# A two-layer hybrid decoder on one core: small products placed singly among large ones, lambda computed later, the rotation fed from a copy, and the compressed weights split by VectorE

## The chip, the core and the metric

The kernel runs on one core of a Trainium2 chip. A core has TensorE (PE, with the weight loads shown apart as PEld), VectorE (DVE), ScalarE (ACT), GpSimd (POOL) and SyncE (SP), which issues the transfers; matrix products are written to PSUM, everything else lies in SBUF. The metric is the device time in microseconds of one execution; less is better.

## The reference

Two layers; in each, a normalised input h is projected once, and three mixers work on the pieces: (A) sparse attention with compressed, selected and window branches, (B) differential attention with two softmax maps a head and a learned lambda, (C) a chunked spatial-gating unit. Their outputs are projected, gated and merged, then a SwiGLU feed-forward follows.

```python
q_a, kv_a, g_a, q_b, k_b, v_b, uv_c = jnp.split(h @ w_in[l], IN_OFFSETS, axis=-1)
# A: compressed branch, then selected blocks and the window (both see every earlier key here: 512 tokens)
p_c = masked_softmax(einsum(q, kc) * scale, cmp_end <= t);  o_cmp = p_c @ vc
out = gb[..., 0:1] * o_cmp + gb[..., 1:2] * o_slc + gb[..., 2:3] * o_win
# B
lam = exp(sum(lq1 * lk1)) - exp(sum(lq2 * lk2)) + lambda_init
o = rmsnorm((p[:, :, 0] - lam * p[:, :, 1]) @ v, subln_g) * (1.0 - lambda_init)
# C
u * (tril(w_s) @ rmsnorm(v) + b_s)
# merge and feed-forward
x = x + (gates_a * (o_a @ w_a) + gates_b * (o_b @ w_b) + gates_c * (o_c @ w_c)) @ w_out
x = x + (silu(h @ w1) * (h @ w3)) @ w2
```

Sizes: 512 tokens, D_MODEL 1024, 8 heads of 64 in two groups for A, 4 double heads for B, feed-forward width 2816, float32.

## The kernel before

Every large product is done in three parts (`mm3`, lines 184 to 186): weights and activations are each split into a rounded high part and the rest, and high x high, low x high, high x low are summed in one PSUM bank, 128 weights columns by 512 tokens each. The V projections run the other way round (`tm`, lines 224 to 226), with 280 or 512 columns. Weights come in chunks of 128 x 1024; `chunk` and `ahead` load them five ahead and split them two ahead: high part by ScalarE (line 163), low part by VectorE (line 166), or by GpSimd for 512 columns of a chunk during the gate products.

The small products are those of the mixers: in the selected and window attention (`nsa`) logits `sA` (lines 878 and 879), transposes of the probabilities `sB` (line 936, 128 columns, two or four at a time), products with V `sC` (lines 958 and 969); in the differential attention (`diff`) the same three (lines 878, 1050, 1061); in the spatial gating `prod` (line 764); in the compressed softmax (`cmp_soft`) the logits `s0` (line 812) and transposes `s4` (line 849). 

The order of work is written by `run`. A list of tasks (projections, gates, branches, feed-forward) yields after each three-part product with an estimate of its time, 650 ns. Two lanes of generators (lane 0: rotation tables, compression, spatial gating, compressed softmax, lambda; lane 1: `nsa` and `diff`) are given that time and step until they have used it up; each step emits its instructions at once and yields a weight. `later` postpones work by a number of ticks, `later_ns` by estimated time. Below this the framework may still move instructions on an engine. Each engine works through its queue in order.

Four banks' names matter: PSUM tiles tagged `g` (three banks, large products), `s` (two, logits and gating), `t` (two, transposes and compressed logits) and `o` (one). A tile's bank is free again when its last reader is done. `rope_pair` rotates a projection: `fa` and `fb` multiply the two halves in PSUM by cosine and sine (lines 663, 664, 673, 674) and, for the sparse attention's queries, keep a raw copy (lines 668, 677, 679); the two halves of QA1 use the copy on VectorE at line 679. `lambdas` (lines 461 to 472) computes lambda, half of the merge biases and a scale, for both layers.

## Time and profile before

| what | value |
|---|---|
| median of 3 runs | 1770.16 us (1769.95 to 1770.19) |
| the profiled execution's own time | 1770.18 us |
| its span, first to last instruction | 1768.3 us |
| granted TensorE clock, mean | 0.999 |
| TensorE products, busy | 1755.5 us, 99%, 8436 records |
| VectorE, ScalarE, GpSimd busy | 968.9, 751.4, 354.0 us |
| DMA | 205.78 MB, mean 116 GB/s |
| TensorE waiting for the raw copy (line 679) | 2.5 us in 2 waits |

Rows of the timeline read: start in us from the span's start, length, engine, line, operation, output <- inputs, shape, count, and in brackets the idle time before it with what ended it. PE is a product, PEld the load of its stationary operand. The ends of products are modelled: 0.39 us for 512 columns, while the next one starts sooner. The list of waits reads: who waited, for whom, us in all, times, the longest.

### The profile page before, as it was taken

What the parts mean: (1) busy time and instruction counts of PE and PEld (TensorE: products, weight loads), DVE (VectorE), ACT (ScalarE), POOL (GpSimd) and SP (SyncE); (2) the same over time, 40 slices, a digit from 0 to 9 for tenths busy, and PEclk for the clock granted to TensorE, in tenths of its full rate; (3) what the DMA queues carried; (4) which work ended last, traced back from release to release, by engine and by line L of the source; (5) the groups of instructions that cost most, each with busy time, mean ns of one, the idle gap of its engine ahead of it and who ended that gap; (6) DMA issues with size and microseconds to landing.
All of it is one profiled execution on the core that took longest, in us unless ns stands there. A gap on an engine that the chain in (4) does not pass through costs nothing.

```text
span 1768.3 us, 22696 instructions
## 1 busy us (share of the span) xinstructions
PE 1755.5 (99%) x8436; PEld 1465.0 (83%) x8436; DVE 968.9 (55%) x1774; ACT 751.4 (42%) x1317; POOL 354.0 (20%) x355
## 2 busy tenths in 40 slices
PE   9999999999999999999999999999999999999998
PEld 7888888888888888888888888888888888888887
DVE  6877665665644444433366786746656444444223
ACT  6557663444333332222244576634533333322222
POOL 0244332444120000000012343214430200000000
PEclk9999999999999999999999999999999999999999
DMA  7571126532322222223344612255413232222221
GB/s 259 190 221 68 54 72 185 173 120 90 113 96 96 96 95 96 96 99 125 109 145 146 220 47 68 80 171 161 149 66 114 95 107 96 96 95 96 100 101 50
DMA packets 67726, 205.78 MB, mean 116 GB/s; under 512 B 8992, under 2 KB 9376, under 8 KB 67616
## 3 DMA queue, kind: packets, MB, share of 16 engines
q1 hardware_dynamic: 67472, 204.29, 34.6%
q8 instruction: 67, 1.10, 0.3%
q14 instruction: 43, 0.35, 0.1%
q10 hardware_dynamic: 144, 0.04, 0.0%
HBM read 185.29 MB, written 19.01 MB: 116 GB/s over the span
## 4 chain that ended last, share of the span: by engine, by line
PE 97%; DVE 1%; ACT 1%; DMA 0%; issue 0%; POOL 0%; SPq 0%; DVEq 0%; ACTq 0%; POOLq 0%
PE ps_g L184 26%; PE ps_g L185 26%; PE ps_g L186 26%; PE ps_o L958 2%; PE ps_t L936 2%; PE ps_s L879 2%; PE ps_g L224 2%; PE ps_s L878 2%; PE ps_g L225 2%; PE ps_g L226 2%; PE ps_o L1061 1%; DVE wl L166 1%; PE ps_o L226 1%; PE ps_o L224 1%; PE ps_o L225 0%; PE ps_t L1050 0%
## 5 line engine op out<-in xcount | busy, mean ns | idle before, releaser
L163 ACT ACTIVATE wh<-wr 128x1024 fp32r<-128x1024 f32 (+2 forms) x320 | 315.4, 989 | 654.2 <-PE ps_g L186 351.7
L184 PE MATMUL ps_g<-xg,wh 128*128 128x512 f32 x1400 | 553.8, 396 | 0.0
L185 PE MATMUL ps_g<-xg,wl 128*128 128x512 f32 x1400 | 546.8, 391 | 0.0
L186 PE MATMUL ps_g<-xg,wh 128*128 128x512 f32 x1400 | 546.2, 390 | 0.1
L166 DVE TENSOR_TENSOR wl<-wr,wh 128x1024 fp32r<-128x1024 f32 (+1 forms) x308 | 367.5, 1195 | 234.8 <-ACT wh L163 231.3
L186 PEld LDWEIGHTS ps_g<-xg,wh 128*128 128x128 f32 x1400 | 262.8, 188 | 56.2 <-DVE xg L283 1.0
L184 PEld LDWEIGHTS ps_g<-xg,wh 128*128 128x128 f32 x1400 | 263.2, 188 | 50.4 <-ACT xg L280 0.5
L185 PEld LDWEIGHTS ps_g<-xg,wl 128*128 128x128 f32 x1400 | 263.3, 188 | 49.0 <-DVE wl L290 0.3
L869 ACT ACTIVATE e<-e,nm 128x384 f32<-128x384 f32 (+2 forms) x192 | 107.2, 559 | 89.0 <-DVE nm L867 85.0
L184 PE MATMUL ps_g<-act,wh 128*128 128x512 f32 (+1 forms) x374 | 141.2, 378 | 0.0
L185 PE MATMUL ps_g<-act,wl 128*128 128x512 f32 (+1 forms) x374 | 140.8, 376 | 0.0
L186 PE MATMUL ps_g<-act,wh 128*128 128x512 f32 (+1 forms) x374 | 140.8, 376 | 0.0
L497 POOL TENSOR_TENSOR acc<-acc,sq 128x512 f32<-128x512 f32 x18 | 29.3, 1626 | 433.6 <-ACT sq L496 433.6
L919 POOL TENSOR_SCALAR e<-e,sm,ga 128x128 f32<-128x128 f32 (+3 forms) x128 | 82.1, 652 | 111.8 <-DVE sm L915 88.7
L867 DVE CUSTOM_DVE_ANT_0 e<-ps_s,con 128x384 f32<-128x384 f32 (+2 forms) x192 | 90.8, 483 | 22.3 <-PE ps_s L879 20.7
L1202 DVE TENSOR_TENSOR fb<-ps_g,R 128x512 f32<-128x512 f32 x44 | 30.4, 691 | 129.1 <-PE ps_g L186 129.1
L166 POOL TENSOR_TENSOR wl<-wr,wh 128x512 fp32r<-128x512 f32 x48 | 72.6, 1513 | 117.7 <-ACT wh L163 117.7
L1193 DVE TENSOR_TENSOR fa<-ps_g,R 128x512 f32<-128x512 f32 x44 | 30.4, 691 | 95.7 <-PE ps_g L186 95.7
L186 PEld LDWEIGHTS ps_g<-act,wh 128*128 128x128 f32 x374 | 70.3, 188 | 13.0
L184 PEld LDWEIGHTS ps_g<-act,wh 128*128 128x128 f32 x374 | 70.3, 188 | 12.9
L185 PEld LDWEIGHTS ps_g<-act,wl 128*128 128x128 f32 x374 | 70.4, 188 | 12.8
L945 DVE TENSOR_TENSOR pt<-ps_t,pt 128x512 fp32r<-128x512 f32 (+1 forms) x96 | 56.7, 597 | 27.4 <-ACT pt L937 27.2
(248 smaller groups left out, 2474.2 us busy)
## 6 DMA issues: line engine op xcount, KB each, us to landing
wr<-in_wst SPq DMA_DIRECT2D x266, 512.0 KB, 3.3
rp_d<-pc SPq DMA_DIRECT2D x112, 128.0 KB, 3.6
wr<-in_wst SPq DMA_DIRECT2D x52, 256.0 KB, 2.6
q<-rp_d SPq DMA_DIRECT2D x16, 512.0 KB, 5.9
kh<-rp_d SPq DMA_DIRECT2D x24, 256.0 KB, 5.8
xT<-in_xT SPq DMA_DIRECT2D x7, 512.0 KB, 6.2
kl<-rp_d SPq DMA_DIRECT2D x12, 256.0 KB, 6.8
xtok<-in_xtok SPq DMA_DIRECT2D x4, 512.0 KB, 8.7
```

The lines of the kernel that those rows point to most:

```text
L163: nc.scalar.activation(h[:, :w], t[:, :w], AF.Copy)
L166: eng.tensor_tensor(lo[:, a:b], t[:, a:b], h[:, a:b].bitcast(F32), op=OP.subtract)
L184: nc.tensor.matmul(out, wh[:, c], xh[:, ts], start=first, stop=False)
L185: nc.tensor.matmul(out, wl[:, c], xh[:, ts], start=False, stop=False)
L186: nc.tensor.matmul(out, wh[:, c], xl[:, ts], start=False, stop=last)
L224: nc.tensor.matmul(o, x[k][:, 0, ts], wh[:, sl], start=(k == 0), stop=False)
L225: nc.tensor.matmul(o, x[k][:, 0, ts], wl[:, sl], start=False, stop=False)
L226: nc.tensor.matmul(o, x[k][:, 1, ts], wh[:, sl], start=False, stop=(k == KT - 1))
L867: nc.vector.tensor_tensor_reduce(out=e[:, :n], in0=s[:, :n], in1=self.mask[:, S - n:], scale=-0.125, scalar=3e38, op0=OP.add, op1=OP.min, ...
L869: nc.scalar.activation(e[:, :n], e[:, :n], AF.Exp, bias=nm, scale=-1.0, accum_out=sm)
L919: nc.gpsimd.tensor_scalar(e[:, :n], e[:, :n], sm[:, h:h + 1], self.ga[:, i, b:b + 1], op0=OP.mult, op1=OP.mult)
L945: nc.vector.tensor_tensor(lo, pt, hi.bitcast(F32), op=OP.subtract)
```

## The change

The diff makes five edits.

1. `mm3` becomes a generator that yields after each of its products (`BIG` = 650/3 ns), and so do `tm`, `prod`, `s0`, `s4`, both `sB`, and in `diff` `sC` and the first logits. The last part of the second layer's feed-forward calls `mm3` without these stops. A yield of a tuple counts time but is no tick (`tick(..., step)`), so work postponed by ticks is due as before. With it lanes can put one small product between two large ones. The weights that lanes yield elsewhere are cut so that a unit's sum is about the same.
2. `lambdas` is divided: biases and scale (`scales`) come with the rotation tables, lambda itself goes behind the first compressed softmax in lane 0; what needed it (gates of C before) becomes KB1.
3. In `fb`, for QA1, the raw copy comes first, and the two products read the copy in SBUF instead of PSUM.
4. In `cmp_soft` the high part of the compressed weights is copied by VectorE in `s5`, just ahead of the low part, and no longer by ScalarE in `s4`.
5. Weights of steps change (W_NSA, W_DIFF shares, 1300 for lambda).

```diff
--- before.py
+++ after.py
@@ -32,6 +32,7 @@
 W_NSA, W_DIFF, LAG = 470, 1200, 4
+BIG = 650 / 3
 WARM = 14
@@ -117,8 +118,9 @@

-    def tick(self, ns=0):
-        self.now += 1
+    def tick(self, ns=0, step=1):
+
+        self.now += step
         self.clock += ns
@@ -182,7 +184,9 @@
         nc.tensor.matmul(out, wh[:, c], xh[:, ts], start=first, stop=False)
+        yield BIG,
         nc.tensor.matmul(out, wl[:, c], xh[:, ts], start=False, stop=False)
+        yield BIG,
         nc.tensor.matmul(out, wh[:, c], xl[:, ts], start=False, stop=last)
@@ -198,14 +202,14 @@
                 outs[m] = self.bank(tag)
-            self.mm3(outs[m], w, x, k, k, k == 0, k == K - 1)
+            yield from self.mm3(outs[m], w, x, k, k, k == 0, k == K - 1)
             if (late and ((m == 0 and k == 5) or (m and k == K - 1))) or (not late and k == 3):
...
                 evacs[m](outs[m])
-            yield 650
+            yield BIG

...
@@ -447,12 +453,27 @@

+    def scales(self):
+
+        nc = self.nc
+        first = len(nc.cur_bb.bb.instructions)
+        self.bh, self.sub = [], []
+        for l in range(L):
+            bh = self.const(f"bh{l}", [P, 24])
+            nc.vector.tensor_scalar(bh, self.par[l][:, P_BM:P_BM + 24], 0.5, None, op0=OP.mult)
+            self.bh.append(bh)
+            sub = self.const(f"sub{l}", [P, 1])
+            nc.vector.tensor_scalar(sub, self.par[l][:, P_SUB:P_SUB + 1], 0.2 + 0.6 * math.exp(-0.3 * l), None,
+                                    op0=OP.mult)
+            self.sub.append(sub)
+        self.holds.append((first, len(nc.cur_bb.bb.instructions)))
+
     def lambdas(self):
...
         lq = self.lq.rearrange("p (l f d) -> p l f d", l=L, f=4)
-        self.nlam, self.bh, self.sub = [], [], []
+        self.nlam = []
         for l in range(L):
@@ -465,14 +486,8 @@
             self.nlam.append(nl)
-            bh = self.const(f"bh{l}", [P, 24])
-            nc.vector.tensor_scalar(bh, self.par[l][:, P_BM:P_BM + 24], 0.5, None, op0=OP.mult)
-            self.bh.append(bh)
-            sub = self.const(f"sub{l}", [P, 1])
-            nc.vector.tensor_scalar(sub, self.par[l][:, P_SUB:P_SUB + 1], 1.0 - li, None, op0=OP.mult)
-            self.sub.append(sub)
         self.holds.append((first, len(nc.cur_bb.bb.instructions)))
-        yield 300
+        yield 1300

@@ -670,13 +685,13 @@
             t2, t3 = self.t2("t2"), self.t2("t3")
+            if raw == 1:
+                nc.vector.tensor_copy(st["raw"][:, 1, :], ps)
+                ps = st["raw"][:, 1, :]
             nc.vector.tensor_tensor(t2, ps, self.sinR, op=OP.mult)
             nc.vector.tensor_tensor(t3, ps, self.cosR, op=OP.mult)
-            if raw is not None:
-                if raw == 0:
-                    nc.scalar.activation(st["raw"][:, 1, :], ps, AF.Copy)
-                else:
-                    nc.vector.tensor_copy(st["raw"][:, 1, :], ps)
+            if raw == 0:
+                nc.scalar.activation(st["raw"][:, 1, :], ps, AF.Copy)
             o1, o2 = st["t1"], st["t4"]
@@ -763,7 +778,8 @@
                                  start=True, stop=True)
-            return ps
+                yield BIG,
+            pss[t] = ps

@@ -788,8 +804,8 @@
             if t < TT:
-                pss[t] = prod(t)
-                yield 1300
+                yield from prod(t)
+                yield 450
                 tmps[t] = mix(t, pss.pop(t))
...
@@ -847,15 +864,18 @@
                 nc.tensor.transpose(pt[:, t * P:(t + 1) * P], st["ef"][:, t, :], self.ident)
-            pc = self.PcT[g] = self.t4("pcT", [P, 2, S], F32R)
-            nc.scalar.activation(pc[:, 0, :], pt, AF.Copy)
+                yield BIG,
+            self.PcT[g] = self.t4("pcT", [P, 2, S], F32R)

...
             pc = self.PcT[g]
+            nc.vector.tensor_copy(pc[:, 0, :], st["pt"])
             nc.vector.tensor_tensor(pc[:, 1, :], st["pt"], pc[:, 0, :].bitcast(F32), op=OP.subtract)

-        for w, f in (((2600 * (g == 0), lambda: None), (1300, s0), (1300, s1), (1300, s2), (2600, ex)), ((2600, s3), (2600, s4), (1300, s5)))[part]:
-            f()
+        for w, f in (((2600 * (g == 0), lambda: None), (450, s0), (1300, s1), (1300, s2), (2600, ex)), ((2600, s3), (450, s4), (1300, s5)))[part]:
+            parts = f()
+            if parts is not None:
+                yield from parts
             yield w
@@ -934,6 +954,7 @@
                     nc.tensor.transpose(pt[:, j - 2 * part, h, :], E[2 * v + h][:, j * P:(j + 1) * P], self.ident)
+                    yield BIG,
             nc.scalar.activation(hi, pt[:, 0:len(js)], AF.Copy)
@@ -1000,16 +1021,16 @@
                 sA(u)
-            yield W_NSA
+            yield W_NSA * 0.6
             w = u - b
...
             if w % 2 and ok(w):
-                sB(w // 2, 0)
+                yield from sB(w // 2, 0)
             elif w % 2 == 0 and ok(w - 2):
-                sB(w // 2 - 1, 1)
+                yield from sB(w // 2 - 1, 1)
             if w % 2 == 0 and ok(w - 4):
                 sC(w // 2 - 2)
-            yield W_NSA
+            yield W_NSA / 4
         self.ensure("oa")
@@ -1023,7 +1044,12 @@
             n = (i + 1) * P
-            s = self.logits(q2[c][:, j], kh[c][:, j, :n], kl[c][:, j, :n], i)
+            ts = slice(i * P, n)
+            s = self.bank("s")
+            nc.tensor.matmul(s[:, :n], q2[c][:, j, ts], kh[c][:, j, :n], start=True, stop=False)
+            if i == 0:
+                yield BIG,
+            nc.tensor.matmul(s[:, :n], q2[c][:, j, ts], kl[c][:, j, :n], start=False, stop=True)
             E[u, j] = self.soft(s, (i + 1) * P, i)
...
@@ -1104,18 +1132,18 @@
             if ok(u):
-                sA(u, 0)
-            yield W_DIFF
+                yield from sA(u, 0)
+            yield W_DIFF * 0.75
             if ok(u):
-                sA(u, 1)
+                yield from sA(u, 1)
             if ok(u - 2):
                 sM(u - 2)
-            yield W_DIFF
+            yield W_DIFF * 0.75
             if ok(u - 3):
-                sB(u - 3)
+                yield from sB(u - 3)
             if ok(u - 4):
-                sC(u - 4)
-            yield W_DIFF
+                yield from sC(u - 4)
+            yield W_DIFF * 0.5
         if p == 1:
@@ -1172,7 +1200,7 @@
             if m < 8:
-                add("g%s%d" % (B, m), [("g" + br, m)], lambda i0, m=m: gate(i0, m), need=need[1:])
+                add("g%s%d" % (B, m), [("g" + br, m)], lambda i0, m=m: gate(i0, m))
             if m >= lead:
...
@@ -1422,11 +1451,11 @@
         add("V", [("v", c) for c in range(3)], g_v)
-        self.merge_tasks(add, l, "c", True, False, ["sgu", "lambda"])
+        self.merge_tasks(add, l, "c", True, False, ["sgu"])
         add("KB0", [("KB0", "A"), ("KB0", "B")], g_rope("KB0"), need=["rows1"])
...
         add("vb", [("vb", c) for c in range(4)], lambda i0: self.tm(i0, self.xg, self.vb_evac, range(0, 9, 2), 512))
-        add("KB1", [("KB1", "A"), ("KB1", "B")], g_rope("KB1"))
+        add("KB1", [("KB1", "A"), ("KB1", "B")], g_rope("KB1"), need=["lambda"])
         add("QB1", [("QB1", "A"), ("QB1", "B")], g_rope("QB1"))
@@ -1464,14 +1493,16 @@
                     yield 1300
+                self.scales()
+                yield 300
             X.append(("tables", ["u30"], tables))
...
         X.append(("softA0", ["QA0%d" % l], lambda: self.cmp_soft(0, 0)))
+        X.append(("cmpv", ["wv3%d" % l], lambda: self.cmp_aux("v")))
+        X.append(("softB0", ["V%d" % l], lambda: self.cmp_soft(0, 1)))
         if l == 0:
             X.append(("lambda", [], self.lambdas))
-        X.append(("cmpv", ["wv3%d" % l], lambda: self.cmp_aux("v")))
-        X.append(("softB0", ["V%d" % l], lambda: self.cmp_soft(0, 1)))
         for part in range(2):
...
@@ -1534,7 +1567,9 @@
             for c in f(i0):
-                self.tick(c)
+                part = isinstance(c, tuple)
+                c = c[0] if part else c
+                self.tick(c, not part)
                 for j in range(len(lanes)):
```


Where the order moves, by engine and place. VectorE at the start of the V projection of layer 0, before (`t<-ps_g` are the products of the rotation, `raw` the copy, `wl` the low part of a weight chunk, `ex` and `nl` belong to lambda, `hg` to the compression of values):

```order
L166 TENSOR_TENSOR wl<-wr,wh 128x840
L461 ISA junk,ex_1078<-lq 128x64
L461 ISA ex_1078 128x1
L469 TENSOR_SCALAR bh_1085<-par_63 128x24
L472 TENSOR_SCALAR sub_1087<-par_63 128x1
```
```order
L466 SCALAR_TENSOR_TENSOR nl_1083<-ex_1078 128x1
L466 SCALAR_TENSOR_TENSOR nl_1094<-ex_1089 128x1
L673 TENSOR_TENSOR t_1120<-ps_g,sinR 128x512
L674 TENSOR_TENSOR t_1121<-ps_g,cosR 128x512
L679 COPY raw<-ps_g 128x512
L607 TENSOR_TENSOR hg<-ps_s,ctmp 64x256
L166 TENSOR_TENSOR wl<-wr,wh 128x840
```

Eight more rows of the same block stand between the two pieces. Now, at the same place:

```order
L168 TENSOR_TENSOR wl<-wr,wh 128x840
L689 COPY raw<-ps_g 128x512
L691 TENSOR_TENSOR t_1106<-raw,sinR 128x512
L692 TENSOR_TENSOR t_1107<-raw,cosR 128x512
L622 TENSOR_TENSOR hg<-ps_s,ctmp 64x256
L168 TENSOR_TENSOR wl<-wr,wh 128x840
```

The copy, last reader of QA1's bank before, is its only reader and stands right behind the weight split; the lambda block is gone from here.

TensorE where the second compressed softmax is transposed (`con,ce`, lines 849 and 866) and the probabilities' transposes (`con,e`) follow, before:

```order
L849 MATMUL ps_t<-con,ce 128x128 x4
L184 MATMUL ps_g<-xg,wh 128x512
L185 MATMUL ps_g<-xg,wl 128x512
L186 MATMUL ps_g<-xg,wh 128x512
L184 MATMUL ps_g<-xg,wh 128x512
L185 MATMUL ps_g<-xg,wl 128x512
L936 MATMUL ps_t<-con,e 128x128 x4
L186 MATMUL ps_g<-xg,wh 128x512
L936 MATMUL ps_t<-con,e 128x128 x4
```

And now, from just ahead of the last of the four transposes on:

```order
L188 MATMUL ps_g<-xg,wl 128x512
L866 MATMUL ps_t<-con,ce 128x128
L956 MATMUL ps_t<-con,e 128x128
L190 MATMUL ps_g<-xg,wh 128x512
L956 MATMUL ps_t<-con,e 128x128
L186 MATMUL ps_g<-xg,wh 128x512
L956 MATMUL ps_t<-con,e 128x128
L188 MATMUL ps_g<-xg,wl 128x512
L190 MATMUL ps_g<-xg,wh 128x512
L186 MATMUL ps_g<-xg,wh 128x512
L188 MATMUL ps_g<-xg,wl 128x512
L956 MATMUL ps_t<-con,e 128x128 x2
```

Four transposes in a row became four with a large product or another transpose between each; the pair in the last row is the first to need the bank that the `con,ce` transposes filled.

VectorE where lambda now stands, among the softmaxes of `nsa` (`e,nm<-ps_s` reads the logits); before and then now:

```order
L867 ISA e,nm<-ps_s,con 128x384
L867 ISA nm 128x1
L1129 TENSOR_TENSOR gt<-ps_g,R 128x512
L915 RECIPROCAL sm_1455<-sm_1455 128x2
L867 ISA e,nm<-ps_s,con 128x512
L867 ISA nm 128x1
```
```order
L482 ISA junk,ex_1451<-lq 128x64
L482 ISA ex_1451 128x1
L935 RECIPROCAL sm_1421<-sm_1421 128x2
L487 SCALAR_TENSOR_TENSOR nl_1449<-ex_1444 128x1
L887 ISA e,nm<-ps_s,con 128x512
L887 ISA nm 128x1
L487 SCALAR_TENSOR_TENSOR nl_1456<-ex_1451 128x1
```

The ten rows of lambda stand in this queue ahead of, and between, the softmaxes of two units of 512 keys.

More of the change, by code (lines that the diff above doesn't have):

```diff
@@ L224, in tm @@
                     nc.tensor.matmul(o, x[k][:, 0, ts], wh[:, sl], start=(k == 0), stop=False)
+                    yield BIG * n / 512,
                     nc.tensor.matmul(o, x[k][:, 0, ts], wl[:, sl], start=False, stop=False)
+                    yield BIG * n / 512,
                     nc.tensor.matmul(o, x[k][:, 1, ts], wh[:, sl], start=False, stop=(k == KT - 1))
-                    yield 650 * n / 512
+                    yield BIG * n / 512
                 if t == 0:
@@ L1063, in sC @@
                                  start=(j == 0), stop=(j == i))
+                yield BIG,
             if i == TT - 1:
@@ L1225, in ffn2 @@
                 self.ahead(i0 + c)
-            self.mm3(ps, w, self.act, pos, k, k == 0, k == FT - 1)
+            yield from self.mm3(ps, w, self.act, pos, k, k == 0, k == FT - 1)
             if k == FT - 1:
                 evac(ps)
-            yield 650
+            yield BIG
     def fin_x(self, k, ts=slice(0, S)):
@@ L1270, in ffn2_tail @@
                     self.ahead(i0 + c)
-                self.mm3(ps, w, self.act, pos, k, k == 0, k == FT - 1, ts)
+                for _ in self.mm3(ps, w, self.act, pos, k, k == 0, k == FT - 1, ts):
+                    pass
                 if k == FT - 1:
@@ L1519, in step @@
                 w = next(c[1])
-                self.tick(w if j else 0)
+                part = isinstance(w, tuple)
+                w = w[0] if part else w
+                self.tick(w if j else 0, not part)
                 return w
```

2 lines of the change are left out of this document (added).

## The prediction

> **What bounds the kernel now.** I read the page first, then the list of who waited for whom on TensorE, then the timeline of TensorE at three kinds of place.
>
> ```profile
> span 1768.3 us, 22696 instructions
> PE 1755.5 (99%) x8436; PEld 1465.0 (83%) x8436; DVE 968.9 (55%) x1774; ACT 751.4 (42%) x1317; POOL 354.0 (20%) x355
> PE 97%; DVE 1%; ACT 1%; DMA 0%; issue 0%; POOL 0%; SPq 0%; DVEq 0%; ACTq 0%; POOLq 0%
> ...
> PE ps_g L224 <- DVE raw L679: 2.5, 2, 1.9
> ...
> PE ps_t L936 <- DVE pcT L855: 0.9, 2, 0.4
> PE ps_s L764 <- DVE stmp L770: 0.6, 1, 0.6
> ```
>
> TensorE's own instruction stream is the bound from end to end: 97% of the chain that ended last is PE. Waits for other engines in mid-kernel add up to 2.5 + 0.9 + 0.6 = 4.0 us. So there are two questions only: does the new order make a product cheaper on TensorE, and do these 4 us go?
>
> The busy share says nothing on the first, since a product's modelled 0.39 us overlaps its neighbour. Starts do. A free stream of large products (88 starts in a row, the first and last shown; the second fence's rows are TensorE's products and weight loads around one small product standing alone, the third a run of four, all from the timeline):
>
> ```profile
> 560.19 0.39 PE L184 MATMUL ps_g<-xg,wh 128*128 128x512 f32 x1
> ...
> 579.91 0.39 PE L184 MATMUL ps_g<-xg,wh 128*128 128x512 f32 x1
> ```
> ```profile
> 390.98 0.40 PE L186 MATMUL ps_g<-oa,wh 128*128 128x512 f32 x1
> 391.22 0.27 PE L1050 MATMUL ps_t<-con,e 128*128 128x128 f32 x1
> 391.25 0.48 PE L184 MATMUL ps_g<-oa,wh 128*128 128x512 f32 x1
> 391.56 0.40 PE L185 MATMUL ps_g<-oa,wl 128*128 128x512 f32 x1
> 391.79 0.39 PE L186 MATMUL ps_g<-oa,wh 128*128 128x512 f32 x1
> 392.02 0.39 PE L184 MATMUL ps_g<-oa,wh 128*128 128x512 f32 x1
> ...
> 391.22 0.19 PEld L184 LDWEIGHTS ps_g<-oa,wh 128*128 128x128 f32 x1
> 391.33 0.19 PEld L185 LDWEIGHTS ps_g<-oa,wl 128*128 128x128 f32 x1
> ```
> ```profile
> 161.48 0.39 PE L186 MATMUL ps_g<-oc,wh 128*128 128x512 f32 x1
> 161.71 0.60 PE L936 MATMUL ps_t<-con,e 128*128 128x128 f32 x4
> 162.06 0.48 PE L878 MATMUL ps_s<-kh,q 128*128 128x512 f32 x1
> 162.38 0.39 PE L879 MATMUL ps_s<-kl,q 128*128 128x512 f32 x1
> ```
>
> A large product costs (579.91 - 560.19)/87 = 0.2267 us. The lone small one: from 390.98 to 391.56 lie two large and one small, 0.58 us, so the small one costs 0.58 - 0.453 = 0.127. The four: from 161.48 to 162.38 lie two large and four small, 0.90, so (0.90 - 0.453)/4 = 0.112 each. The reason is in the loads: the load for the next large product (391.22) begins when the small product starts and not sooner, and the load behind it follows 0.11 us later. A small product thus lasts as long as one weight load, 0.11 us, alone or in a row; the slack under a large product is not used, because only one load runs ahead.
>
> **The change part by part.**
>
> *Small products one at a time.* Counted in TensorE's order, the stretches of narrower products between products of 512 columns go from 279 to 620: 341 more. The total of products stays 8256 instructions, so only the price of a stretch counts. By the rows above alone against in a run it is 0.127 - 0.112 = 0.015; starts are read to 0.01 and a run pays its entry once too, so I take 0.012: 341 x 0.012 = **+4.1 us**. Bounds: 0 (rounding), and 0.022, since the starts 391.56, 391.79, 392.02 stand 0.23 apart and not 0.2267, twice up to 0.005 more: 341 x 0.022 = 7.5. The f32 products that the trace records twice (attention weights times V in the differential attention, the spatial gating) have no lone row; they lie nearest to the lone transpose, are priced as it is, and keep the same bounds.
>
> *Rotation from a copy, and lambda leaving.* Both act at the start of the V projection (line 224), which needs the PSUM bank of QA1's second half:
>
> ```profile
> 114.31 0.29 PE L225 MATMUL ps_o<-wl,xg 128*128 128x280 f32 x1
> 116.54 0.40 PE L224 MATMUL ps_g<-wh,xg 128*128 128x280 f32 x1 [1.94 <-DVE raw L679]
> 116.78 0.29 PE L225 MATMUL ps_g<-wl,xg 128*128 128x280 f32 x1
> ...
> 112.36 1.03 DVE L166 TENSOR_TENSOR wl<-wr,wh 128x840 fp32r<-128x840 f32 x1 [1.64 <-ACT wh L163]
> 113.31 0.22 DVE L461 CUSTOM_DVE_ANT_0 junk<-lq 128x64 f32<-128x64 f32 x1
> 114.61 0.68 DVE L673 TENSOR_TENSOR t<-ps_g,sinR 128x512 f32<-128x512 f32 x1
> 115.81 0.68 DVE L679 COPY raw<-ps_g 128x512 f32<-128x512 f32 x1
> ```
> ```profile
> 988.92 0.29 PE L226 MATMUL ps_o<-wh,xg 128*128 128x280 f32 x1
> 989.17 0.29 PE L225 MATMUL ps_o<-wl,xg 128*128 128x280 f32 x1
> 990.01 0.40 PE L224 MATMUL ps_g<-wh,xg 128*128 128x280 f32 x1 [0.55 <-DVE raw L679]
> ...
> 987.13 1.03 DVE L166 TENSOR_TENSOR wl<-wr,wh 128x840 fp32r<-128x840 f32 x1 [1.63 <-ACT wh L163]
> ```
>
> Products of 280 columns stand 0.13 apart (988.92 to 989.17 are two). The first stall costs 116.54 - 114.31 - 0.13 = 2.10, and 0.11 more at the product behind it, whose load also starts late (0.24 instead of 0.13); layer 1 loses 990.01 - 989.17 - 0.13 = 0.71. Now the copy comes right behind the weight split, and the lambda block (113.31 to 114.61, 1.30 us) is gone: copy done at 113.39 + 0.68 = 114.07, needed at 114.31 + 0.13 = 114.44. Layer 1: 988.16 + 0.68 = 988.84, needed at 989.30. Both stalls go whole, with 0.4 us to spare: 2.10 + 0.11 + 0.71 + some 0.1 behind the second = **-3.0 us**. Late next would be the second weight chunk of V, whose split ended at 113.39, well ahead. Bound on the other side: if the split ahead of the copy comes 1 us late, 0.6 of each stall stays, so -1.8.
>
> *Compressed weights split by VectorE.* The transposes of the next probabilities wait for the bank that the compressed softmax holds:
>
> ```profile
> 188.25 0.48 PE L186 MATMUL ps_g<-xg,wh 128*128 128x512 f32 x1
> 189.18 0.66 PE L936 MATMUL ps_t<-con,e 128*128 128x128 f32 x4 [0.44 <-DVE pcT L855]
> ...
> 187.80 0.60 ACT L851 ACTIVATE pcT<-ps_t 128x512 fp32r<-128x512 f32 x1
> 188.43 0.69 DVE L855 TENSOR_TENSOR pcT<-ps_t,pcT 128x512 fp32r<-128x512 f32 x1 [0.46 <-ACT pcT L851]
> ```
>
> From the large product to the transposes 0.93 us pass where 0.32 is usual behind a run (162.06 to 162.38): 0.61 lost, in each layer (the list counts two such waits), 1.2 in all. ScalarE reached this copy late, behind other work; now VectorE does it, 0.60 + 0.69 = 1.3 us of its time in a row. In the new order, between the last transpose into this bank and the one that needs it back stand 6 large products and 3 transposes, 6 x 0.2267 + 3 x 0.11 = 1.7 us; the bank is due 0.3 (a transpose's own length) + 1.3 = 1.6 us after. Just in time if VectorE is free, so I take **-0.9**; bounds -1.2 and 0 (VectorE late by 0.6).
>
> *Spatial gating.*
>
> ```profile
> 86.96 1.16 PE L764 MATMUL ps_s<-sw,v 128*128 128x128 f32 x8 [0.64 <-DVE stmp L770]
> ...
> 86.23 0.68 DVE L770 TENSOR_TENSOR stmp<-ps_s,sw 128x512 f32<-128x512 f32 x1
> ```
>
> VectorE's order is unchanged here, but on TensorE the waiting product now stands one large product later (0.23), and the four that follow are spread. I take **-0.4**, bounds -0.6 (the wait) and 0.
>
> *Lambda's new place.* Its 1.3 us of VectorE and two exponentials of ScalarE now stand among the selected-attention softmaxes, with the logits of the next units queued behind them and TensorE waiting for those PSUM banks only when two units are open. Cover is VectorE's idle time, 45% over the span. I take **+0.3**, bounds 0 and 1.3. The rotation products now read a copy in SBUF, off the path.
>
> Sum: 4.1 - 3.0 - 0.9 - 0.4 + 0.3 = +0.1. The profiled execution took 1770.18 us (span 1768.3), the median of the runs is 1770.16, so the base is the same either way: **1770.3 us**. With all bounds: 0 - 3.0 - 1.2 - 0.6 + 0 = -4.8, and 7.5 - 1.8 + 0 + 0 + 1.3 = +7.0.
>
> **The rivals.**
>
> 1. *A lone product costs no more than one in a run, and every named wait goes.* Then -4.8: **1765.4**. For it: the difference of 0.015 rests on starts read to 0.01, and the list of waits is short and addressed whole. Against: the rows behind the lone product are stretched too.
>
> 2. *The large products hide the small ones.* If two loads ran ahead, a lone product would cost its streaming alone. From 512 and 280 columns, (0.2267 - 0.13)/232 = 0.00042 per column, so 128 columns take 0.13 - 152 x 0.00042 = 0.066, 0.046 less than now. For some 440 products that stand alone in the new order this gives -20, with the waits **1746**. Against it: the load at 391.22, which did not start before the small product did. The Trainium skill ("TensorE: Matmul & The Clock Gate", section "Architectural detail: the array is 16× 32×32, not 1× 128×128") has TensorE's queue pull weight loads ahead of products in flight; read as several loads ahead this is the rival, read as one ahead it is the row.
>
> 3. *Slower: the exposed load behind each lone product.* After a small product the load of the second large product starts 0.11 late (391.33), and a weight split that was ready just in time is now waited for.
>
> ```profile
> 359.48 0.27 PE L1050 MATMUL ps_t<-con,e 128*128 128x128 f32 x1
> 359.59 0.19 PEld L185 LDWEIGHTS ps_g<-oa,wl 128*128 128x128 f32 x1 [0.20 <-DVE wl L166]
> 359.93 0.40 PE L186 MATMUL ps_g<-oa,wh 128*128 128x512 f32 x1
> ```
>
> Here the load came 0.11 after the small product instead of with it. If one lone product in nine meets this, the price is 0.012 + 0.11/9 = 0.024, 341 x 0.024 = 8.2, and the sum +4.2: **1774.4**. It decides from 0.022 each, where the sum passes +3.5. For it: the rows. Against: the lone product at 391.22 in the same stage met none, and splits so late are seen where branch weights of 512 columns follow a gate.
>
> **How the numbers follow.** A measurement of this kernel tells about 0.2%, 3.5 us, from no change. Forecast (the sum within 3.5 us) 0.54; rival 1 0.20, rival 2 0.04, rival 3 0.22. Hence faster 0.24, same 0.54, slower 0.22. The range takes in rivals 1 and 3 and most of the bounds, 1764.5 to 1775.5; below it lies rival 2 and the far end of 1, above it the upper bounds together.
>
> **What would show it.** In the changed profile: L224 no longer waits for the raw copy (2.5 to under 0.3); the transposes wait for pcT under 0.3; a lone transpose between large ones takes 0.12 to 0.13 from start to start, with its successor's load at its own start. Wrong I would be if lone products took 0.07 (rival 2), if the two starts behind one stood much over 0.23 apart (rival 3), or if a new row of over 1 us stood in TensorE's list of waits.

## The result, and the profile after

The changed kernel takes **1790.8 us** (median, 1789.9 to 1791.1) against 1770.1 for the kernel before, run beside it: ratio 1.0112, 95% interval 1.0100 to 1.0124. It is slower by 20.7 us. The forecast was no change, 1770.3, with a range to 1775.5: wrong in sign and size. The profiled execution took 1791.11 us, its span 1789.3.

From the page of the changed kernel: span, busy time, the chain that ended last, and the list of waits (who waits, for whom, us in all, times, the longest):

```profile
span 1789.3 us, 22684 instructions
PE 1764.9 (99%) x8436; PEld 1461.1 (82%) x8436; DVE 985.7 (55%) x1778; ACT 747.4 (42%) x1315; POOL 350.9 (20%) x355
PE 92%; DVE 3%; ACT 2%; issue 1%; POOL 1%; DMA 1%; SPq 0%; DVEq 0%; ACTq 0%
...
PE ps_s L898 <- DVE nm L887: 5.1, 4, 2.2
PE ps_t L956 <- DVE pt L966: 4.8, 10, 1.1
PE ps_s L1049 <- DVE nm L887: 2.7, 4, 1.0
PE ps_g L186 <- ACT xg L286: 1.2, 2, 0.9
...
PE ps_g L188 <- DVE wl L168: 0.5, 1, 0.5
...
PE ps_s L779 <- DVE stmp L786: 0.4, 1, 0.4
```

The waits that the change addressed are gone: the V projection no longer waits for the raw copy (2.5 before), nothing waits for the compressed weights (0.9), and the spatial gating waits 0.4 instead of 0.6. In their place stand three rows that the kernel before did not have, 5.1 + 4.8 + 2.7 = 12.6 us. (A fourth new row, 1.2 us for `xg`, lies in the first 10 us of the program; in the other kernels below it is between nothing and 1.4.) The three are of one kind: TensorE wants a PSUM bank back that VectorE has not read yet. `nm` (line 887) is the softmax's reading of the logits, so lines 898 and 1049 are the logits of the selected and the differential attention; `pt` (line 966) is the low part of the transposed probabilities, so line 956 is the next transposes. The busy shares hardly moved, and VectorE is idle 45% of the span as before: the share told nothing of this. The chain shows it, with PE at 92% where it had 97%.

The longest wait, from the timeline of the changed kernel (TensorE's logits, VectorE's products for the compressed values and its third reading of the logits, GpSimd's weight split):

```profile
129.84 0.28 PE L898 MATMUL ps_s<-kh,q 128*128 128x256 f32 x1
131.24 0.39 PE L190 MATMUL ps_g<-xg,wh 128*128 128x512 f32 x1
133.81 0.47 PE L898 MATMUL ps_s<-kh,q 128*128 128x512 f32 x1 [2.18 <-DVE nm L887]
...
128.94 2.18 DVE L667 TENSOR_SCALAR VCS<-vcs,con 128x256 fp32r<-128x256 f32 x4
131.04 0.68 DVE L854 TENSOR_REDUCE csm<-ce 128x16 f32<-128x512 f32 x1
133.36 0.29 DVE L887 CUSTOM_DVE_ANT_0 e<-ps_s,con 128x128 f32<-128x128 f32 x1
...
129.04 1.40 POOL L168 TENSOR_TENSOR wl<-wr,wh 128x512 fp32r<-128x512 f32 x1 [8.90 <-ACT wh L165]
```

The same place before:

```profile
130.53 0.28 PE L878 MATMUL ps_s<-kh,q 128*128 128x256 f32 x1
133.94 0.40 PE L878 MATMUL ps_s<-kh,q 128*128 128x512 f32 x1
...
128.35 1.13 DVE L652 TENSOR_SCALAR VCS<-vcs,con 128x256 fp32r<-128x256 f32 x4
132.25 0.29 DVE L867 CUSTOM_DVE_ANT_0 e<-ps_s,con 128x128 f32<-128x128 f32 x1
...
129.72 1.43 POOL L166 TENSOR_TENSOR wl<-wr,wh 128x512 fp32r<-128x512 f32 x1 [9.81 <-ACT wh L163]
```

The first two logits fill one `s` bank each, and VectorE empties them in turn, two readings a bank; the third logits need the first bank, which is free after the third reading. Two things differ. The third logits are asked for sooner: 6 products of 512 columns stand between them and the second ones in the new order, 12 and four transposes in the old (3.41 us from 130.53 to 133.94). And VectorE is later: its third reading ends at 133.65, before at 132.54. Its four products took 1.13 us and were done at 129.48, ahead of GpSimd's split (129.72); now they take 2.18 us and run beside it. The view of that tile gives the shortest, median and longest of its eight, in ns, first of the changed kernel, then of the one before:

```profile
L667 DVE TENSOR_SCALAR VCS<-vcs,con x8: 341/346/1391, 128.9 to 1014.7; 128x256 fp32r<-128x256 f32 x8
```
```profile
L652 DVE TENSOR_SCALAR VCS<-vcs,con x8: 341/346/349, 128.4 to 1002.6; 128x256 fp32r<-128x256 f32 x8
```

One product took 1391 ns instead of 346: it began at 129.20 and ended at 130.59, just behind GpSimd's split, which ran from 129.04 to 130.44. In the other layer the four take 2.18 us too. The Trainium skill ("SBUF — State Buffer", section "SBUF: two separate sides") says that GpSimd and some kinds of VectorE's instructions share one pair of SBUF ports as an exclusive lock, held for a whole instruction by whoever starts first, while the other waits. The one product that stood still for a whole split agrees with the lock; on who gets it see the last section.

The wait costs 133.81 - 131.24 - 0.23 = 2.34 us. Then comes more. Busy share and granted clock of TensorE in the microseconds behind it (changed kernel):

```profile
134.00:135.00 1.00, 1.00 (x4) 0.59 0.98 389
135.00:136.00 1.00, 1.00 (x4) 0.50 0.61 242
136.00:137.00 1.00, 1.00 (x4) 0.50 0.19 74
137.00:138.00 1.00, 1.00 (x6) 0.70 0.01 4
138.00:139.00 1.00, 1.00 (x8) 1.00 0.00 0
```

The third column is the clock: it drops to half. 0.41 + 0.50 + 0.50 + 0.30 = 1.7 us are lost to it, so this place costs 4.0 us in each layer (in the second, TensorE waits 2.17 us at 1017.68, and the clock falls behind it too).

### The profile page after: what moved, and what is told of

Same layout as the page of the kernel before. It is cut to its first block, busy times and chain, and to the rows that moved or that the text cites. A ratio compares the mean times of both kernels' runs of the same rounds, so it can differ in the third digit from the quotient of the medians.

```text
span 1789.3 us, 22684 instructions
## 1 busy us (share of the span) xinstructions
PE 1764.9 (99%) x8436; PEld 1461.1 (82%) x8436; DVE 985.7 (55%) x1778; ACT 747.4 (42%) x1315; POOL 350.9 (20%) x355
## 4 chain that ended last, share of the span: by engine, by line
PE 92%; DVE 3%; ACT 2%; issue 1%; POOL 1%; DMA 1%; SPq 0%; DVEq 0%; ACTq 0%
PE ps_g L186 25%; PE ps_g L188 25%; PE ps_g L190 25%; PE ps_o L979 2%; PE ps_t L956 2%; PE ps_g L232 1%; PE ps_g L230 1%; PE ps_g L228 1%; PE ps_o L1088 1%; PE ps_s L898 1%; PE ps_s L899 1%; ACT wh L165 1%; DVE wl L168 1%; PE ps_o L230 0%; PE ps_o L232 0%
## 5 line engine op out<-in xcount | busy, mean ns | idle before, releaser
L186 PE MATMUL ps_g<-xg,wh 128*128 128x512 f32 x1400 | 560.6, 400 | 1.9 <-ACT xg L286 1.2
L188 PE MATMUL ps_g<-xg,wl 128*128 128x512 f32 x1400 | 556.6, 398 | 0.5 <-DVE wl L168 0.5
L190 PE MATMUL ps_g<-xg,wh 128*128 128x512 f32 x1400 | 556.0, 397 | 0.1
L168 DVE TENSOR_TENSOR wl<-wr,wh 128x1024 fp32r<-128x1024 f32 (+1 forms) x308 | 361.9, 1177 | 229.8 <-ACT wh L165 229.2
L956 PE MATMUL ps_t<-con,e 128*128 128x128 f32 x320 | 79.8, 275 | 4.8 <-DVE pt L966 4.8
L188 PEld LDWEIGHTS ps_g<-act,wl 128*128 128x128 f32 x374 | 70.4, 188 | 12.8
L186 PEld LDWEIGHTS ps_g<-act,wh 128*128 128x128 f32 x374 | 70.4, 188 | 12.8
```

The lines of the kernel that those rows point to most:

```text
L168: eng.tensor_tensor(lo[:, a:b], t[:, a:b], h[:, a:b].bitcast(F32), op=OP.subtract)
L186: nc.tensor.matmul(out, wh[:, c], xh[:, ts], start=first, stop=False)
L188: nc.tensor.matmul(out, wl[:, c], xh[:, ts], start=False, stop=False)
L190: nc.tensor.matmul(out, wh[:, c], xl[:, ts], start=False, stop=last)
L956: nc.tensor.transpose(pt[:, j - 2 * part, h, :], E[2 * v + h][:, j * P:(j + 1) * P], self.ident)
```

## The experiments

**The theories.** A: the lone products cost about what was forecast; the loss is in new waits for banks, made by the finer order and its step weights. B: the lone products themselves are dear; 20.7 us and the 3.9 saved, over 341 more stretches, would be 0.072 each. C: lambda's new place, or the compressed weights' split on VectorE, delays the softmaxes. Later came D: VectorE is late because GpSimd's weight splits now collide with its work. "Above" and "under" are medians against the kernel before in the same series. Its median was 1771.4 in the first series (the first four experiments) and 1770.1 to 1770.4 in all others, so distances from different series compare to about 1 us only.

### Edits 2 to 4 alone

```diff
 # before.py, with lambda moved, rotation from the copy, and in s5:
+            nc.vector.tensor_copy(pc[:, 0, :], st["pt"])
```

> The kernel before with edits 2 to 4 alone (lambda moved, rotation from the copy, compressed weights split by VectorE); small products stay in runs and the step weights stay as before. Theory A (a lone product costs 0.012 us, and the 20.7 us come from new waits for PSUM banks that the finer order and its step weights make): the two waits of line 224 and the two for the compressed weights go and nothing comes, 1770.1 - 3.0 - 0.9 = 1766.2, range 1765.5 to 1768. Theory B (the lone products themselves are dear): the same, 1766. Theory C (lambda or the split on VectorE delays the softmaxes, and that is what is lost): 1785 or more, with rows of TensorE waiting for the nm row of the softmax.

1768.9 against 1771.4: 2.5 us under, ratio 0.9988 (0.9979 to 0.9998). Theory C falls: in the old order these edits cost nothing. How much they gain is less sure: in this series 8 of the 20 executions of the kernel before took 1769.9 to 1770.4 us and 12 took 1771.3 to 1772.1, and against the lower group the gain is 1.2.

### Single products and step weights alone

```diff
 # after.py
-    edits 2 to 4
+    as before.py
```

> The changed kernel with edits 2 to 4 undone, so only the single products and the step weights are new. Theory A: the old waits come back on top, 1790.8 + 3.9 = 1794.7, range 1792 to 1797, and TensorE still waits 2.2 us at the third logits of the selected attention. Theory B: the same. Theory C: near before, 1770 to 1776.

1787.2, 15.8 above, ratio 1.0085 (1.0068 to 1.0102); TensorE waits up to 2.2 us at the third logits as it does with the edits. So the loss belongs to edits 1 and 5. But it is 4.9 us less than with edits 2 to 4 (3.6 by the two medians themselves), and theory A wanted 3.9 more: the parts do not add.

### The selected attention as before

```diff
-            yield W_NSA * 0.6
+            yield W_NSA
-            yield W_NSA / 4
+            yield W_NSA
-                    yield BIG,      # in sB
```

> The changed kernel with the selected attention as before: its transposes in runs again and both of its step weights 470; everything else stays single. Stretches of narrow products in TensorE's order: 481 instead of 620. Theory A: the waits of its logits (5.7 us and some 3.3 us of halved clock) and of its transposes (6.6 us) go, and 139 x 0.012 = 1.7: 1790.8 - 5.7 - 3.3 - 6.6 - 1.7 = 1773.5, range 1771 to 1777. Theory B: 20.7 us and the 3.9 saved, over 341 stretches, are 0.072 each; 139 x 0.072 = 10.0: 1780.8, and the range 1779 to 1783. Theory C: 1788 to 1791.

1773.7, 2.3 above, ratio 1.0014 (1.0005 to 1.0023): 17 to 18 us less than the whole change. Theory A had 1773.5, B 1780.8.

### Only the empty steps padded

In `nsa` a unit's two steps yield 470 x 0.6 and 470 / 4, plus 217 for each transpose. A step without transposes therefore lasts 400 ns of the lane's time where it lasted 940. This kernel pads such steps at the ends of each call of `nsa`: of its 39 steps the first five and the last two. (Eight more have an empty second set of transposes and stay at 400.)

```diff
             elif w % 2 == 0 and ok(w - 2):
                 yield from sB(w // 2 - 1, 1)
+            else:
+                yield W_NSA * 1.15
```

> The changed kernel in which only those steps of the selected attention that issue no transposes yield as much time as before (470 x 1.15 more), so that its third logits come 15 products of 512 columns after the second ones, not 6; every small product stays single (650 stretches instead of 620). Theory A: the wait at the start of the selected attention (2.2 us, each layer) and the halved clock behind it (1.7 us, each layer) go, the waits of the transposes stay: 1790.8 - 8.0 + 30 x 0.012 = 1783.2, range 1781 to 1785.5. Theory B: 30 more lone products at 0.072: 1793. Theory C: 1790 to 1792.

1777.7, 6.3 above, ratio 1.0035 (1.0022 to 1.0048), with more lone products than the change has. Its list of waits:

```profile
PE ps_s L1051 <- DVE nm L887: 3.8, 4, 1.4
PE ps_t L866 <- DVE pt L966: 2.2, 2, 1.1
...
PE ps_t L866 <- DVE ce L861: 1.0, 2, 0.5
```

The waits of the selected logits are gone, and so are those of the selected transposes, which were expected to stay: 14.4 us less (13.1 by the two medians themselves), not 7.6. Why the later waits went as well is not shown. The pad does not spread the later units: in TensorE's order 97 large products lie from the fifth logits of the first call to its last in the change, and 96 here. They only fall at another time against the queues of VectorE and GpSimd. Theory B, which allowed for no gain, falls. (The expectation's 15 products, like the 14 of a later one, is a miscount: in the two orders 13 and 12 large products and four transposes lie between the second and the third logits.)

### The differential attention as before

```diff
-            yield W_DIFF * 0.75        # twice, and W_DIFF * 0.5
+            yield W_DIFF               # three times; no yield inside sA, sB, sC
```

> The changed kernel with the differential attention as before (its logits, transposes and products with V in runs, each step weight 1200). 510 stretches of narrow products instead of 620. Theory A (waits for PSUM banks; a lone product itself 0.003 to 0.012 us): the waits of the differential logits for the softmax go, 4.0 us with what follows them, and 110 x 0.003 to 0.012: 20.7 - 4.0 - 0.3 to 1.3, that is 15.4 to 16.4 us above before. Theory B (lone products dear, 0.07 each): 20.7 - 7.9 = 12.8 above before.

1784.9, 14.5 above, ratio 1.0078 (1.0063 to 1.0093): 6.2 less than the change, between the two theories. Here the trace shows why runs of this kernel do not add up. Up to that stage the order is the changed kernel's own, on every engine, but a wait of 1.1 us is missing, in each layer. Changed kernel, then this one:

```profile
191.69 1.85 DVE L168 TENSOR_TENSOR wl<-wr,wh 128x512 fp32r<-128x512 f32 x1
191.72 1.28 POOL L168 TENSOR_TENSOR wl<-wr,wh 128x512 fp32r<-128x512 f32 x1
193.47 1.28 DVE L966 TENSOR_TENSOR pt<-ps_t,pt 128x512 fp32r<-128x512 f32 x2
194.20 0.33 PE L956 MATMUL ps_t<-con,e 128*128 128x128 f32 x1 [1.08 <-DVE pt L966]
```
```profile
191.77 0.68 DVE L168 TENSOR_TENSOR wl<-wr,wh 128x512 fp32r<-128x512 f32 x1
191.80 1.80 POOL L168 TENSOR_TENSOR wl<-wr,wh 128x512 fp32r<-128x512 f32 x1
192.37 0.68 DVE L966 TENSOR_TENSOR pt<-ps_t,pt 128x512 fp32r<-128x512 f32 x1
193.11 0.33 PE L956 MATMUL ps_t<-con,e 128*128 128x128 f32 x1
```

The two halves of a weight split become ready together, on VectorE and on GpSimd, 0.03 us apart. One of them takes its usual time, and the other is held up for most of that time. When VectorE loses, the low parts behind it are 1.1 us late, and TensorE waits.

### Lambda alone put back, and the split on ScalarE alone put back

```diff
 # after.py, lambda ahead of the V projection again
-        add("KB1", ..., need=["lambda"])
+        self.merge_tasks(add, l, "c", True, False, ["sgu", "lambda"])
```

> The changed kernel with lambda alone put back ahead of the V projection. The single products without edits 2 to 4 stood 15.8 us above before, with them 20.7, so one of the edits costs some 4.9 in the finer order. If it is lambda's place among the softmaxes: 16 above before, and fewer or shorter waits of the selected logits. If it is not: 20 to 22 above before.

```diff
 # after.py, s4
+            nc.scalar.activation(pc[:, 0, :], pt, AF.Copy)
```

> The changed kernel with the high part of the compressed weights copied by ScalarE again. If the split on VectorE is what costs 4.9 us in the finer order (its 0.60 us more stand ahead of the low parts of the probabilities, for which the transposes wait): 16 to 17 above before, and TensorE's wait for those low parts falls from 4.8 us in 10 waits toward the 2.7 us in 6 that the kernel without edits 2 to 4 showed. If not: 20 to 22.

15.8 above (ratio 1.0086, 1.0071 to 1.0101) and 17.2 above (1.0100, 1.0085 to 1.0115). By the numbers as stated, both would be at fault, for 4.9 and 3.5 us of the same 4.9. The traces say neither. With lambda back, the two waits of 1.1 us at the transposes of 194.20 and 1078.10 are missing, and VectorE's splits ahead of them took 0.84 and 0.68 us; but lambda is computed in the first layer only. With the split back, the first of them is missing, and in the traced execution the clock stayed up, where the change lost 3.4 us to it. What moved is which collisions VectorE loses. Lambda itself costs nothing that can be seen: in the changed kernel the wait at 133.81, in lambda's layer, and its twin at 1017.68 both idle TensorE 2.2 us, and lambda's rows begin at 142.7, behind the first.

### Both attentions padded

```diff
-            yield W_DIFF * 0.75
+            yield W_DIFF               # the first two steps of a unit
```

> The kernel with padded empty steps of the selected attention (6.3 us above before) in which also the first two steps of each unit of the differential attention yield 1200, not 900; every small product stays single (630 stretches, 465 of them one product). Theory A: the waits of the differential logits for the softmax go (4.4 us with what follows), the waits of the compressed transposes (3.9) stay: 6.3 - 4.4 = 1.9 above before, range 0.5 to 3.5. Theory B: no change, 6.3 above before.

1774.2, 3.9 above, ratio 1.0021 (1.0011 to 1.0030): 2.4 less than with the selected attention padded alone, and the waits of the differential logits are gone from the list. 1.9 had been expected.

### The short steps alone, products in runs

The mirror of the padding: the kernel before, nothing spread, in which the same seven steps of a call are cut.

```diff
-            yield W_NSA                # twice
+            yield W_NSA * (1 if some else 0.6)
+            yield W_NSA * (1 if some else 0.25)   # some: the step has transposes
```

> The kernel before, every small product still in runs (273 stretches), in which only those steps of the selected attention that issue no transposes yield 0.6 and 0.25 of their weight, as in the change. Its third logits then stand 6 products of 512 columns behind the second, as in the change (14 before). Theory A (the loss is the order's pace, not the single products): TensorE waits 2.2 us at the third logits in each layer, with the clock halved behind it in some executions: 4.5 to 8 us above before, a few more if the later units meet waits too. Theory B (lone products): no difference from before, 0 within 1.5.

1777.9, 7.5 above, ratio 1.0044 (1.0028 to 1.0059), with no product newly set singly. The pace is a cause by itself. But the time came out right for a wrong reason: the wait at the third logits is 0.2 us here, not 2.2, and the loss is spread over transposes, logits and weight splits. In this trace VectorE's four products took 1.13 us, ahead of GpSimd's split. So pace alone made no long wait here. But one more thing differs: VectorE's product `ce` (0.68 us), which stands ahead of the second reading of the logits in the kernel before and in the change, has moved behind the third (131.82; the third reading starts at 131.61). In the old place it would have made this wait some 0.6 us longer (an estimate: in the change the next reading starts 0.61 behind `ce`).

### Only the attentions single

```diff
 # after.py, both attentions padded; in s0, s4 and prod:
-                    yield BIG,
```

> The changed kernel with both attentions paced as in the padded kernels, and the compressed softmax and the spatial gating in runs as before: 568 stretches instead of the 279 of edits 2 to 4 alone, 388 of them one product, and hardly a wait left that those edits alone do not have. What it stands above them (they were 2.5 us under before) is the price of the lone products. Theory A: 289 x 0.003 to 0.010 = 0.9 to 2.9, so 1.6 under before to 0.4 above, plus any wait that the list still shows. The forecast's 0.012 each would give 3.5, so 1.0 above. Theory B: 289 x 0.07 = 20, so 18 above before.

1775.4, 5.0 above, ratio 1.0029 (1.0017 to 1.0040), above the expected range. It does not price the lone products, since waits came back: 1.2 us at the gating, 1.2 and 0.7 at the transposes, 0.7 at the V projection.

### Lambda's move alone

```diff
 # before.py
-            X.append(("lambda", [], self.lambdas))     # ahead of cmpv
+            X.append(("lambda", [], self.lambdas))     # behind softB0
```

> The kernel before with lambda's move alone (edit 2). By the forecast's terms: the wait at the V projection of layer 0 loses lambda's 1.30 us of its 2.2, that of layer 1 stays at 0.55 idle, and lambda's new place costs 0 to 1.3, taken as 0.3: 1.0 under before, range 1.3 under to equal.

1770.0 against 1770.4, ratio 0.9997 (0.9988 to 1.0006); 1.0 under had been expected. The wait at the V projection fell from 2.5 to 1.2 us as expected, but a weight split is now waited for 0.6 us at 72.71, during the compression of the keys. The small gain lies inside the expected range, and inside the noise.

### No weight split on GpSimd

```diff
-POOLED = {"g": 512}
+POOLED = {}
```

> The changed kernel with no weight split given to GpSimd: VectorE splits all 1024 columns of the gate chunks. If the 1.25 us waits for the low parts of the probabilities (194.20 and 1078.10 in the changed kernel's trace) come from a VectorE split that takes 1.85 us instead of 0.68 beside GpSimd's: no 512-column split over 0.9 us, no such wait, and 2 to 3 us less where VectorE's longer splits (1.27 for 1024 columns) do not cost as much elsewhere. If VectorE's load is what counts: 3 us or more above the changed kernel.

1783.2, 12.8 above, ratio 1.0074 (1.0060 to 1.0088): 7.9 less than the change, where 2 to 3 had been expected, though VectorE has more to do. The 1.1 us waits are gone, and the waits of the selected logits fell from 5.1 to 2.1 us: GpSimd had a part there too, or the order of VectorE's queue, in which `ce` has moved behind the third reading here as well.

### One split taken from GpSimd

```diff
-            self.pool_cols = POOLED.get(n[0], 0)
+            self.pool_cols = 0 if n[:3] == "gC0" else POOLED.get(n[0], 0)
```

TensorE's order is instruction for instruction that of the changed kernel. On VectorE, the 512 columns that it now splits itself come behind the first `csm`, and the first three readings of the logits stand sooner, the second and third now ahead of `ce` (0.68 us).

> The changed kernel in which the weight split that falls due during the first gate of C (one chunk a layer) is done by VectorE alone and not shared with GpSimd; TensorE's order is the same, instruction for instruction. Theory D (VectorE is late at the third selected logits because GpSimd's split collides with its products for the compressed values): those four products take 1.13 us instead of 2.18, the wait there falls from 2.2 to 0.7 us in each layer and the clock stays up: 20.7 - 2 x 1.5 - 2 x 1.65 = 14.4 above before, range 13 to 17.5. Theory A alone (pace): VectorE gets 0.6 us more to do, the wait stays 2.2: 20 to 22.

1784.2, 14.0 above, ratio 1.0072 (1.0057 to 1.0087); theory D had 14.4 (a fit that is in part luck, as the rows show). From this kernel's view of the tile and its timeline:

```profile
L667 DVE TENSOR_SCALAR VCS<-vcs,con x8: 345/346/349, 129.0 to 1010.0; 128x256 fp32r<-128x256 f32 x8
```
```profile
132.37 0.47 PE L898 MATMUL ps_s<-kh,q 128*128 128x512 f32 x1 [0.70 <-DVE nm L887]
133.38 0.40 PE L898 MATMUL ps_s<-kh,q 128*128 128x512 f32 x1
```

No product is held up, and the wait is 0.70 us instead of 2.18, though VectorE does 0.68 us more; the clock stayed up. The 1.48 us are not all the collision's: from the start of the four products to the end of the third reading VectorE takes 3.23 us here and 4.71 in the change, and the four products are 1.05 of the difference (1.13 and 2.18). The other 0.43 is its changed order, `ce` gone from ahead of the third reading and the split come in its stead. This kernel is 6.7 us faster than the change: twice 1.5 of wait and twice 1.7 of clock, and small shifts of both signs, of which one is that the 1.1 us wait at 194.20 is missing here too.

### No split on GpSimd, in the old and in the padded order

```diff
 # edits 2 to 4 alone; both attentions padded
-POOLED = {"g": 512}
+POOLED = {}
```

> Edits 2 to 4 alone (2.5 us under before), with no weight split on GpSimd. In that order TensorE waits 3.1 us in mid-kernel at all, so there is little to win: 3.5 under before if the collisions are in it, 1 under to 2 above if VectorE's longer splits (1.27 for 1024 columns) come late behind the gates.

> The kernel with both attentions padded (3.9 us above before, waits 8.1 us) and no weight split on GpSimd. Theory D: its waits of the compressed transposes (1.25 us twice for the low parts of the probabilities, 0.67 twice for the compressed weights) shrink by some 3: 1 above before, range 0.5 under to 2.5 above. Theory A alone: they stay, and 3 to 6 above.

In the old order with edits 2 to 4: 1769.7, 0.5 under, ratio 0.9997 (0.9988 to 1.0005), 2.0 worse than with GpSimd's help, but only 0.8 by the two medians themselves (1769.7 and 1768.9), so nothing is won there and little lost. In the padded order: 1771.5, 1.3 above, ratio 1.0005 (0.9996 to 1.0014), 2.6 better than with it. The waits of the padded kernel without GpSimd's splits, those of its start and its end left out:

```profile
PE ps_g L188 <- DVE wl L168: 0.8, 2, 0.4
PE ps_t L866 <- DVE pt L966: 0.5, 2, 0.3
PE ps_g L186 <- ACT wh L165: 0.5, 1, 0.5
PE ps_s L779 <- DVE stmp L786: 0.4, 1, 0.4
```

All small products stand as singly as in the change (628 stretches, 620 there), and the 20.7 us are down to 1.3: 20.7, then 6.3 with the empty steps of `nsa` padded, 3.9 with `diff` padded too, 1.3 without GpSimd's splits.

**The price of a lone product** can now be taken from a free stretch (both attentions padded, 347.19 to 348.23: three small products and three large ones):

```profile
347.19 0.27 PE L1078 MATMUL ps_t<-con,e 128*128 128x128 f32 x1
...
347.54 0.27 PE L1078 MATMUL ps_t<-con,e 128*128 128x128 f32 x1
...
347.89 0.27 PE L1078 MATMUL ps_t<-con,e 128*128 128x128 f32 x1
...
348.23 0.27 PE L1078 MATMUL ps_t<-con,e 128*128 128x128 f32 x1
```

1.04 / 3 = 0.347 for a pair; less 0.227 for the large one, 0.120, where one in a run took 0.112: 0.008. The whole kernels agree: padded without GpSimd against edits 2 to 4 without GpSimd, 1.8 us for 347 stretches is 0.005, some of it waits; against edits 2 to 4 with GpSimd, 3.8 us for 349 is 0.011 (2.6 and 0.007 by the two medians themselves), some of it waits too.

## Why the prediction was wrong

**The step that failed** is the sentence on the small products: "The total of products stays 8256 instructions, so only the price of a stretch counts." It priced the edit on TensorE alone. The same edit also sets when each logit and each transpose is asked for, and there are only two `s` banks and two `t` banks, which VectorE gives back. No term was made of edit 5, the step weights: a step without transposes went from 940 to 400 ns of the lane's time. TensorE's order showed the third logits moved from 12 large products and four transposes behind the second to 6. In the kernel before, the reading that empties their bank ended at 132.54; a waiting product starts some 0.16 us behind that reading (133.65 and 133.81 in the change, 131.89 and 132.04 in the mirror), so the bank was free at 132.70, and TensorE asked for it at 133.94: 1.24 us to spare. In the change TensorE asks at 131.24 + 0.23 = 131.47, 2.47 us sooner, and the reading ends 1.11 us later. 2.47 + 1.11 - 1.24 = 2.34, the whole wait. Of the 1.11 us, 1.05 are the four products that GpSimd's split held up: it begins 0.1 us behind the first of them (129.04 and 128.94) and no longer after the last. By these figures the sooner asking alone would have cost about 1.3 us, and the collision the other 1.05; that is an estimate, since in both runs that part the two (the mirror and the one split) VectorE's order moved as well.

**Second**, "Cover is VectorE's idle time, 45% over the span" was no cover. VectorE's idle time is a mean; the banks are needed back where it has a row of work queued: in the three microseconds from 131 on, ahead of the wait's end, it was 0.97, 0.93 and 0.87 busy. The sum's upper bound of +7.0 held no new wait of TensorE for a bank beyond lambda's 1.3, so the range could not reach 20.

**The terms one by one.**

- Lone products, +4.1: by the free stretch 341 x 0.008 = 2.7. The mechanism (a lone product lasts as long as a weight load) held; the size was too high by half. The price lies between rival 1 (nothing) and the forecast; rival 2 (hidden altogether) is excluded.
- Rotation and lambda, -3.0, and the compressed weights, -0.9: the waits named are gone. Alone, with lambda's place, these edits gave -2.5 (0.2 to 2.1 per mille under before; 1.2 us against the lower group of that series), against -3.6 forecast.
- Spatial gating, -0.4: the wait fell by 0.2.
- Lambda's place, +0.3: nothing seen.
- Rival 3 had the right sign but another mechanism: it adds 341/9 x 0.11 = 4.2 us of waits for VectorE's weight splits, and the list shows one of 0.5.

**The balance.** To the 20.7 us comes the 2.5 that edits 2 to 4 saved (or 1.2); 2.7 are the lone products. Of the other 20.5, 12.6 are the idle of the three new rows. The 18 waits in them cost a little more than their idle: at 133.81, 2.34 for 2.18. The halved clock takes 2 x 1.7 = 3.4. That leaves some 4.5 us: 1.2 at the program's start, and the rest for those entries, for weight splits that are waited for and for waits too short for the list; their shares were not separated. That a third bank for the logits would have taken their waits away was not tried.

The last condition that the forecast set for itself ("if a new row of over 1 us stood in TensorE's list of waits") was met by all three rows.

## What to carry to other kernels

When an edit changes the order in which work is issued, price the places where a buffer is asked for again, not only the instructions: for each bank, the products between its use and its next use, against the time by which the engine that frees it will be done in its own queue there. When a planner's weights are divided, look at the steps that have nothing to issue: here they shrank to less than half, and padding seven of the 39 steps of a call won back 13 to 14 of 21 us. And where VectorE and GpSimd are given the two halves of one job, they may run one after the other; what stands behind VectorE's half is then late by as much.

## What the runs showed of the hardware

**Collisions decide small differences.** VectorE's 512-column split takes 0.68 us where it is not held up and 1.85 where it is, and which of the two engines is held up is not settled by the order: VectorE started 0.03 us ahead of GpSimd in both kernels above, and lost in one of them. By the recorded starts, then, the first one does not always win. That this is why kernels of nearly the same order differed by up to 5 us is read from their traces and was not tested apart.

**The clock may fall behind a wait of 2 us, and does not always.** With the same wait, the kernel with the split on ScalarE kept its clock:

```profile
133.72 0.47 PE L898 MATMUL ps_s<-kh,q 128*128 128x512 f32 x1 [2.17 <-DVE nm L887]
```
```profile
134.00:135.00 1.00, 1.00 (x6) 1.00 0.94 340
135.00:136.00 1.00, 0.99 (x5) 1.00 0.93 369
```

Three of its four executions took 1787.5 to 1787.6 us and one 1791.4, 3.8 more, which is about what two such falls cost; that the fourth had them is inferred. Even shorter waits can be followed by a fall: with lambda's move alone TensorE waited 0.48 us at 70.67 and 0.59 at 72.71, and then:

```profile
73.00:74.00 1.00, 1.00 (x4) 0.50 0.51 152
74.00:75.00 1.00, 1.00 (x4) 0.50 0.96 365
```

In the old order with edits 2 to 4 and without GpSimd's splits it is one wait of 0.94 us, at 72.32, with the clock at 0.50 from 73 to 76. Both of these traced executions were among the longest of their kernel: 1771.8 us, where the nine others took 1769.4 to 1770.5, and 1771.2, where eight of the ten others took 1769.2 to 1770.2. The distance is about the 1.7 us of one fall. That the two groups of the kernel before, 1.6 us apart, are with and without one such fall is likely by this and not shown, as only an execution of the lower group was traced.

The Trainium skill ("TensorE: Matmul & The Clock Gate", section "What's actually happening") puts the half clock behind an idle window of about 3.4 us, and says that the windows run free of the kernel. The second agrees with a fall that comes in one execution and not in another; on the first the measurement differs, since no wait here was longer than 2.2 us.
